# RMSNorm and matmul on one core: one token layout for loads and stores, a deeper prefetch, and one store cut at row 60

## The chip, the core and the metric

The kernel runs on one core of a Trainium2 chip. The metric is device time in microseconds (us), the median of several executions. "Span" is the length of one execution from its first to its last instruction; the timed figure of the same execution is about 1.8 us above it in every run here (the profiled one of the kernel before: span 210.9, time 212.7). An execution over 1.5% above the fastest of its kernel counts as slow. The engines: TensorE (PE) multiplies, VectorE (DVE) and ScalarE (ACT) do elementwise work, GpSimd (POOL) casts, SyncE (SP) issues transfers, and 16 DMA engines move the data.

## The reference, cut to what matters

```python
x: (16, 1024, 512) float32, gamma: 512 ones, weight: (512, 768) float32
rms = np.sqrt(np.mean(x ** 2, axis=-1, keepdims=True) + eps)
return np.matmul(x / rms * gamma, weight)          # (16, 1024, 768) float32
```

That is 16,384 tokens: 128 tiles of 128 tokens, in 16 groups of eight tiles. 33.6 MB are read and 50.3 MB written, and both TensorE and the DMA engines are nearly full.

## The kernel before

A tile's token sits in a partition, and a DMA of n tiles gives each of the 128 partitions n consecutive tokens. The same cutting of a group serves x and the output:

```python
AHEAD = 20
parts = {0: [1, 2, 1, 2, 2], 1: [4, 4], NG - 2: [4, 4], NG - 1: [2, 2, 2, 1, 1]}   # other groups: [8]
def rows(ap, i):
    return ap[first[i] * P:(first[i] + size[i]) * P, :].rearrange("(p t) d -> p t d", t=size[i])
xin  = ctx.enter_context(tc.tile_pool(name="xin", bufs=5))     # five groups of x
outp = ctx.enter_context(tc.tile_pool(name="out", bufs=3))     # three groups of output
def store(i):
    if i == first[i] + size[i] - 1:
        nc.sync.dma_start(out=rows(out, i), in_=held(o_tiles, first[i], size[i]))
# ... (casts, norms, transposes, matmuls left out)
warm_up(6); cast(0, nc.vector); square(0, ssq[:, 0:1]); transpose_tile(0); warm_up(3)   # start, on one line here
# ...
for j in range(2, NP):
    load_until(2 * j + AHEAD)
    # ... cast, norms, matmuls of tiles 2j and 2j+1, each followed by its store if the stretch is complete
```

All loads and stores are issued by SyncE in program order into one queue, which all 16 DMA engines work off. A store waits on SyncE for its last tile.

Of the kernel before, what the change touches and what calls it, by code (L numbers as in the profile page):

```python
# [18 lines left out]
def kernel(  # L19
# [8 lines left out]
    nc = tc.nc  # L28
    P = 128

    x = x.flatten_outer_dims()
    out = out.flatten_outer_dims()
# [3 lines left out]
    NT = N // P  # L36
    NP = NT // 2
    G = 8
    NG = NT // G
    AHEAD = 20  # L40
    WIDE = 512



    parts = {0: [1, 2, 1, 2, 2], 1: [4, 4], NG - 2: [4, 4], NG - 1: [2, 2, 2, 1, 1]}
    first, size = {}, {}
    for g in range(NG):
        i = g * G
        for n in parts.get(g, [G]):
            for t in range(n):  # L50
                first[i + t], size[i + t] = i, n
            i += n

    def rows(ap, i):
        return ap[first[i] * P:(first[i] + size[i]) * P, :].rearrange("(p t) d -> p t d", t=size[i])

    singles = ctx.enter_context(tc.tile_pool(name="singles", bufs=1))
    xin = ctx.enter_context(tc.tile_pool(name="xin", bufs=5))
# [8 lines left out]
    x_tiles, xb_tiles, tp_tiles, rstd_of, xT_tiles, o_tiles = {}, {}, {}, {}, {}, {}  # L67

    def held(tiles, i, n=1):
        return tiles[i // G][:, i % G:i % G + n, :]  # L70

    def load(i):
        if i // G not in x_tiles:
            x_tiles[i // G] = xin.tile([P, G, D], F32, name="xt")
        nc.sync.dma_start(out=held(x_tiles, i, size[i]), in_=rows(x, i))

    starts = [i for i in range(NT) if first[i] == i]

    def load_until(i):
        while starts and starts[0] < i:  # L80
            load(starts.pop(0))
# [52 lines left out]
    def accumulator():  # L134
        return opsum.tile([P, 2, WIDE], F32, name="ops").rearrange("p a b -> p (a b)")

    def out_tile(i):
        if i // G not in o_tiles:
            o_tiles[i // G] = outp.tile([P, G, O], F32, name="ot")
        return o_tiles[i // G][:, i % G, :]  # L140

    def store(i):
        if i == first[i] + size[i] - 1:
            nc.sync.dma_start(out=rows(out, i), in_=held(o_tiles, first[i], size[i]))

    def matmul(i, k, acc, lo, hi):
        nc.tensor.matmul(out=acc[:, lo:hi], lhsT=xT_tiles[i // 2][:, i % 2, k // 2, :, k % 2], rhs=w_bf[:, k, lo:hi],  # L147
                         start=(k == 0), stop=(k == K - 1))


    def matmuls(i, acc, ks, feed=None):
        for k in ks:
            matmul(i, k, acc, 0, WIDE)
            if feed:
                feed()
            matmul(i, k, acc, WIDE, O)

    def finish_tile(i, acc, engine):
        scale(engine, out_tile(i), acc[:, :O], rstd_of[i])
        store(i)  # L160
# [16 lines left out]
    with tc.manual_schedule():  # L177
# [9 lines left out]
        for h in range(2):  # L187
            nc.sync.dma_start(out=w_f32[:, 2 * h:2 * h + 2, :].rearrange("p c o -> p (c o)"), in_=wv[:, h, :])
        load_until(AHEAD)


        warm = singles.tile([P, WIDE], BF16)
        nc.vector.memset(warm, 0.0)  # L193
# [6 lines left out]
        def warm_up(n):  # L200
            for _ in range(n):
                nc.tensor.matmul(out=spare[:, :WIDE], lhsT=warm[:, :P], rhs=warm, start=True, stop=True)  # L202

        w_bf = singles.tile([P, K, O], BF16)

        def weights(k, engine, lo=0, hi=O):
            scale(engine, w_bf[:, k, lo:hi], w_f32[:, k, lo:hi], g_sb[:, k % 2, k // 2:k // 2 + 1])
# [21 lines left out]
        acc = [accumulator() for _ in range(4)]  # L229
        weights(0, nc.vector, 0, WIDE)  # L230
        weights(0, nc.vector, WIDE, O)
# [26 lines left out]
        for j in range(2, NP):  # L258
            load_until(2 * j + AHEAD)
            if j + 3 < NP:  # L260
# [19 lines left out]
        for i in (NT - 2, NT - 1):  # L280
            for lo, hi, engine in ((0, WIDE, nc.scalar), (WIDE, O, nc.vector)):
                a = accumulator()
                for k in range(K):
                    matmul(i, k, a, lo, hi)
                scale(engine, out_tile(i)[:, lo:hi], a[:, lo:hi], rstd_of[i])
            store(i)
# [35 lines left out]
```

## Time and profile before

| | before |
|---|---|
| median time | 211.38 us at first, 211.45 in the six runs beside the changed kernel |
| last matmul ends | 203.06 us |
| last store has landed, most engines / last engine | 206.7 / 210.0 us |
| end of the span | 210.9 us |

Read the table backwards, and note that the profiled execution was one of the slower ones (212.7 us). The span ends 0.9 us after the last engine, the last engine trails the others by 3.3 us, and the others are done 3.1 us after the last store was issued, at 203.6. The start and the end of TensorE's work, from the chain that ended last in order of time (start, duration, what):

```profile
0.74 2.87 DMA xt<-in_x_dram
...
7.45 1.40 PE ops L202 x6
8.85 2.61 PE ops L147 x16
...
197.41 5.65 PE ops L147 x35
```

The first tile of x lands at 3.61, six dummy matmuls that keep TensorE warm take 1.40 us, the real matmuls begin at 8.85 and the last piece ends at 203.06. The time from issue to landing (last column) of the large transfers:

```profile
out_dram<-ot SPq DMA_DIRECT2D x12, 3072.0 KB, 15.2
xt<-in_x_dram SPq DMA_DIRECT2D x12, 2048.0 KB, 19.6
```

### The profile page before, as it was taken

How to read it: one execution, taken by the hardware profiler on the slowest of the kernel's cores; microseconds unless marked ns; L12 is line 12 of the kernel's file. 1: busy time of each engine (PE TensorE's matmuls, PEld its weight loads, DVE VectorE, ACT ScalarE, POOL GpSimd, SP SyncE). 2: the span in 40 equal slices, each digit the busy share in tenths (PEclk: the TensorE clock that was granted, in tenths of full speed). 3: DMA queues.
4: the chain of work that ended last, by engine and by line, in shares of the span. 5: the costliest groups of instructions: out<-in, count | busy, mean ns of one | idle time of the engine just before them, and what ended most of it. 6: DMA issues, size and time to landing. Idle time of an engine off the chain costs nothing.

```text
span 210.9 us, 3573 instructions
## 1 busy us (share of the span) xinstructions
PE 199.8 (95%) x1272; PEld 138.0 (65%) x1297; DVE 111.6 (53%) x204; ACT 158.3 (75%) x388; POOL 66.2 (31%) x71
## 2 busy tenths in 40 slices
PE   7999999999999999999999999999999999999950
PEld 2466767766666777766667667766676777766620
DVE  2555654565456446645654565456546644654530
ACT  4589787778778877877787778777877887787720
POOL 1165512416233323332331333224143305050000
PEclk9999999999999999999999999999999999999996
DMA  6999999999999999999999999999999999999991
GB/s 228 408 428 423 398 398 420 418 419 431 441 407 427 437 437 412 438 435 406 447 418 441 416 432 438 364 435 429 432 418 437 418 451 383 422 440 378 392 376 78
DMA packets 8070, 85.69 MB, mean 406 GB/s; under 512 B 1138, under 2 KB 1140, under 8 KB 3956
## 3 DMA queue, kind: packets, MB, share of 16 engines
q1 hardware_dynamic: 7776, 85.46, 97.0%
q8 instruction: 10, 0.16, 0.3%
q10 hardware_dynamic: 276, 0.00, 0.1%
q14 instruction: 8, 0.07, 0.1%
HBM read 35.13 MB, written 50.33 MB: 405 GB/s over the span
## 4 chain that ended last, share of the span: by engine, by line
PE 92%; DMA 1%; DVE 1%; ACT 1%; issue 1%
PE ops L147 77%; PE tp L113 13%; DMA xt<-in_x_dram 1%; PE ops L202 1%; DVE ot L132 1%; ACT ot L130 0%; DVE xT L120 0%; ACT jk L90 0%; DVE xb L86 0%; PE tp L224 0%; ACT rms L94 0%; DVE rstd L96 0%
## 5 line engine op out<-in xcount | busy, mean ns | idle before, releaser
L147 PE MATMUL ops<-w_bf,xT 128*128 128x512 bf16 (+1 forms) x999 | 192.5, 324 | 1.4
L147 PEld LDWEIGHTS <-xT 128*128 128x128 bf16 x1024 | 100.2, 98 | 56.2 <-DVE xT L120 0.9
L86 POOL CAST xb<-xt 128x1024 bf16<-128x1024 f32 (+1 forms) x65 | 65.5, 1016 | 121.7 <-DMA xt<-in_x_dram 58.5
L120 DVE COPY xT<-tp 128x1024 bf16<-128x1024 bf16 (+1 forms) x67 | 44.5, 667 | 82.2 <-PE tp L113 82.2
L130 ACT ACTIVATE ot<-ops,rstd 128x768 f32<-128x768 f32 (+1 forms) x65 | 58.1, 894 | 38.6 <-PE ops L147 37.3
L90 ACT ACTIVATE jk<-xt 128x512 bf16<-128x512 f32 x128 | 78.8, 619 | 1.2 <-DMA xt<-in_x_dram 1.2
L113 PE MATMUL tp<-ident_f,xb 128*128 128x128 f32 x256 | 69.1, 275 | 0.4 <-DVE xb L86 0.3
L132 DVE TENSOR_SCALAR ot<-ops,rstd 128x768 f32<-128x768 f32 (+1 forms) x65 | 64.5, 992 | 2.9 <-PE ops L147 2.8
L113 PEld LDWEIGHTS tp<-ident_f,xb 128*128 128x128 f32 x256 | 36.0, 142 | 4.9 <-issue 1.1
L90 ACT ACTIVATION_READ_ACCUMULATOR jk<-xt 128x1 f32 x128 | 24.4, 190 | 0.0
L94 ACT ACTIVATE rms<-ssq,eps_sb 128x2 f32<-128x2 f32 (+1 forms) x64 | 18.9, 295 | 2.0
L96 DVE RECIPROCAL rstd<-rms 128x2 f32<-128x2 f32 (+1 forms) x64 | 9.9, 155 | 3.3 <-ACT rms L94 3.2
L202 PE MATMUL ops<-warm 128*128 128x512 bf16 x15 | 5.7, 531 | 1.2 <-DVE eps_sb L195 1.2
L202 PEld LDWEIGHTS <-warm 128*128 128x128 bf16 x15 | 1.7, 125 | 3.1 <-issue 1.4
L130 ACT ACTIVATE w_bf<-w_f,g_sb 128x768 bf16<-128x768 f32 x2 | 1.9, 936 | 1.4 <-DVE g_sb L226 1.4
L184 ACT ACT_TABLE_LOAD x1 | 1.3, 1283 | 1.8 <-issue 1.8
L86 DVE CAST xb<-xt 128x512 bf16<-128x512 f32 x2 | 1.1, 537 | 2.5 <-DMA xt<-in_x_dram 2.5
L132 DVE TENSOR_SCALAR w_bf<-w_f,g_sb 128x512 bf16<-128x512 f32 (+2 forms) x3 | 1.3, 475 | 0.0
L193 DVE MEMSET warm<- 128x256 uint32 x1 | 0.3, 272 | 0.9 <-PEq L303 0.9
L224 PE MATMUL tp<-ident_f,g_row 2*128 2x2 f32 x2 | 0.4, 265 | 0.3 <-DVE xT L120 0.3
L224 PEld LDWEIGHTS tp<-ident_f,g_row 2*128 2x128 f32 x2 | 0.3, 202 | 0.5 <-DVE xT L120 0.5
masks.py:199 POOL TENSOR_SCALAR_AFFINE_SELECT ident_f<-ident_f 128x128 f32<-128x128 f32 x1 | 0.3, 292 | 0.1
(7 smaller groups left out, 0.8 us busy)
## 6 DMA issues: line engine op xcount, KB each, us to landing
out_dram<-ot SPq DMA_DIRECT2D x12, 3072.0 KB, 15.2
xt<-in_x_dram SPq DMA_DIRECT2D x12, 2048.0 KB, 19.6
out_dram<-ot SPq DMA_DIRECT2D x4, 1536.0 KB, 11.8
out_dram<-ot SPq DMA_DIRECT2D x6, 768.0 KB, 9.4
xt<-in_x_dram SPq DMA_DIRECT2D x4, 1024.0 KB, 14.4
xt<-in_x_dram SPq DMA_DIRECT2D x6, 512.0 KB, 15.2
w_f<-in_weight_dram SPq DMA_DIRECT2D x2, 768.0 KB, 6.0
out_dram<-ot SPq DMA_DIRECT2D x4, 384.0 KB, 9.3
```

Of the source, the lines that this page charges most:

```text
L86: engine.tensor_copy(out=xb_tiles[i // 2][:, i % 2:i % 2 + n, :], in_=held(x_tiles, i, n))
L90: nc.scalar.activation(out=jk, in_=held(x_tiles, i)[:, 0, :], func=AF.Square, accum_out=ssq)
L94: nc.scalar.activation(out=rms[:, :n], in_=ssq[:, :n], func=AF.Sqrt, scale=1.0 / D, bias=eps_sb)
L96: nc.vector.reciprocal(out=rstd[:, :n], in_=rms[:, :n])
L113: nc.tensor.transpose(out=tp_tiles[j][:, t, h, :], in_=words[:, lo:lo + P], identity=ident_f)
L120: nc.vector.tensor_copy(out=dst[:, t:t + n, :], in_=src[:, t:t + n, :])
L130: nc.scalar.mul(out=dst, in_=src, mul=r)
L132: nc.vector.tensor_single_scalar(out=dst, in_=src, scalar=r, op=mybir.AluOpType.mult)
L147: nc.tensor.matmul(out=acc[:, lo:hi], lhsT=xT_tiles[i // 2][:, i % 2, k // 2, :, k % 2], rhs=w_bf[:, k, lo:hi], start=(k == 0), stop=(k == ...
L184: nc.scalar.preload_act_table(AF.Sqrt)
L202: nc.tensor.matmul(out=spare[:, :WIDE], lhsT=warm[:, :P], rhs=warm, start=True, stop=True)
L224: nc.tensor.transpose(out=gp[:, c, :], in_=g_row[:, :, c], identity=ident_f[:2, :2])
```

## The change

Its intent: every group has the same layout (partition p holds tokens 8p to 8p+7 of its group), so loads and stores may be cut differently; the last loads and first stores become larger; loads are issued a group earlier; and one store is divided unevenly over the DMA engines. The core of the diff:

```diff
-    AHEAD = 20
+    AHEAD = 28
+    MID = 5
-    parts = {0: [1, 2, 1, 2, 2], 1: [4, 4], NG - 2: [4, 4], NG - 1: [2, 2, 2, 1, 1]}
+    x_first, x_size = stretches({0: [1, 2, 1, 2, 2], 1: [4, 4]})
+    o_first, o_size = stretches({0: [4, 4], MID: [5, 3], NG - 2: [4, 4], NG - 1: [2, 2, 2, 1, 1]})
-        return ap[first[i] * P:(first[i] + size[i]) * P, :].rearrange("(p t) d -> p t d", t=size[i])
+        return ap.rearrange("(g p t) d -> g p t d", p=P, t=G)[i // G, :, i % G:i % G + n, :]
     def store(i):
-        if i == first[i] + size[i] - 1:
-            nc.sync.dma_start(out=rows(out, i), in_=held(o_tiles, first[i], size[i]))
+        first, n = o_first[i], o_size[i]
+        if i == first + n - 1:
+            uneven = first == MID * G + 5
+            for lo, hi in ((0, 60), (60, P)) if uneven else ((0, P),):
+                nc.sync.dma_start(out=rows(out, first, n)[lo:hi], in_=held(o_tiles, first, n)[lo:hi])
```

More of the change, by code (lines that the diff above doesn't have):

```diff
@@ L39, with stretches, rows @@
     NG = NT // G
-    AHEAD = 20
+    AHEAD = 28
     WIDE = 512
-    parts = {0: [1, 2, 1, 2, 2], 1: [4, 4], NG - 2: [4, 4], NG - 1: [2, 2, 2, 1, 1]}
-    first, size = {}, {}
-    for g in range(NG):
-        i = g * G
-        for n in parts.get(g, [G]):
-            for t in range(n):
-                first[i + t], size[i + t] = i, n
-            i += n
-    def rows(ap, i):
-        return ap[first[i] * P:(first[i] + size[i]) * P, :].rearrange("(p t) d -> p t d", t=size[i])
+    MID = 5
+    def stretches(parts):
+        first, size, i = {}, {}, 0
+        for g in range(NG):
+            for n in parts.get(g, [G]):
+                for t in range(i, i + n):
+                    first[t], size[t] = i, n
+                i += n
+        return first, size
+    x_first, x_size = stretches({0: [1, 2, 1, 2, 2], 1: [4, 4]})
+    o_first, o_size = stretches({0: [4, 4], MID: [5, 3], NG - 2: [4, 4], NG - 1: [2, 2, 2, 1, 1]})
+    def rows(ap, i, n):
+        return ap.rearrange("(g p t) d -> g p t d", p=P, t=G)[i // G, :, i % G:i % G + n, :]
     singles = ctx.enter_context(tc.tile_pool(name="singles", bufs=1))
@@ L74, in load @@
             x_tiles[i // G] = xin.tile([P, G, D], F32, name="xt")
-        nc.sync.dma_start(out=held(x_tiles, i, size[i]), in_=rows(x, i))
-    starts = [i for i in range(NT) if first[i] == i]
+        nc.sync.dma_start(out=held(x_tiles, i, x_size[i]), in_=rows(x, i, x_size[i]))
+    starts = [i for i in range(NT) if x_first[i] == i]
     def load_until(i):
```

## The prediction

> **What bounds the kernel now.** I read the page's busy table first, then its 40 slices, then the chain that ended last, then the stretch after the last matmul, then the DMA issues and who waits for DMA.
>
> ```profile
> PE 199.8 (95%) x1272; PEld 138.0 (65%) x1297; DVE 111.6 (53%) x204; ACT 158.3 (75%) x388; POOL 66.2 (31%) x71
> ...
> PE   7999999999999999999999999999999999999950
> ...
> DMA  6999999999999999999999999999999999999991
> ...
> q1 hardware_dynamic: 7776, 85.46, 97.0%
> ...
> PE 92%; DMA 1%; DVE 1%; ACT 1%; issue 1%
> ```
>
> Two resources are full at once: TensorE from slice 2 to slice 38, the DMA engines from slice 2 to slice 39. The chain names TensorE for 92% of the span, but the last two digits differ: TensorE is at 5 and 0 while DMA is at 9 and 1. The end is therefore a matter of stores.
>
> TensorE's pace is regular. In the chain in order of time four matmuls take 0.65 us and the transpose between fours 0.11, so a tile (eight matmuls, two transposes) takes 2 x (0.65 + 0.11) = 1.52 us and a group of eight 12.15; the stores of eight tiles are issued at 47.29, 59.43, 71.58, the same 12.15. The DMA records give the other pace: a packet is one partition's row of one DMA, 16,384 bytes of x take 611 ns at least (634.9 on average) and 24,576 bytes of output 912 (median). An engine has 8 of each per group: 4.89 + 7.30 = 12.19 us at best, 12.4 on average. So DMA is a little slower than TensorE and the queues carry a backlog.
>
> The cores' work after the last matmul (it ends at 203.06), in stretches; the columns after the engines' busy times are the granted clock, the DMA share of 16 engines, and GB/s:
>
> ```profile
> 199.00:204.00 5.00, 4.04 (x26) 2.21 (x23) 2.12 (x5) 2.27 (x3) 0.00 (x0) 1.00 0.88 361
> 204.00:206.00 2.00, 0.00 (x0) 0.00 (x0) 0.00 (x0) 0.00 (x0) 0.00 (x0) 1.00 0.99 399
> 206.00:207.00 1.00, 0.00 (x0) 0.00 (x0) 0.00 (x0) 0.00 (x0) 0.00 (x0) 1.00 0.39 151
> 207.00:208.00 1.00, 0.00 (x0) 0.00 (x0) 0.00 (x0) 0.00 (x0) 0.00 (x0) 0.85 0.14 55
> 208.00:209.00 1.00, 0.00 (x0) 0.00 (x0) 0.00 (x0) 0.00 (x0) 0.00 (x0) 0.50 0.09 37
> 209.00:210.00 1.00, 0.00 (x0) 0.00 (x0) 0.00 (x0) 0.00 (x0) 0.00 (x0) 0.50 0.04 15
> ```
>
> One sixteenth is 0.06. From 207 on only one to three of the 16 engines still move data; the rest are done. In the packet records the 16 completion marks of the last store are at 206.69 (first), 206.82 (ninth), 208.94, 209.07 and 210.02 (last); the span ends 0.9 us after that. The last engine can be followed back: its rows of the eight-tile stores take 931 to 1025 ns, mostly 954 to 964, where the others take 912 (about 90 of 1,536 packets, one engine's share being 96). It is about 5% slow on every store and carries its lag to the end.
>
> Who waits for DMA:
>
> ```profile
> POOL xb L86 <- DMA xt<-in_x_dram: 58.5, 20, 7.2
> ...
> PEld L147 <- DVE xT L120: 0.9, 2, 0.5
> ...
> ACT ot L130 <- DMA out_dram<-ot: 0.6, 1, 0.6
> ```
>
> GpSimd's casts wait for x 20 times, but nothing of it reaches TensorE: the weight loads waited 0.9 us in all. An output buffer was waited for once, 0.6 us.
>
> **What the Trainium skill says.** "DMA: Bandwidth & Descriptors", section "Why a DMA increments its semaphore by 16 and not by 1": a DMA issued from SyncE runs on the largest k up to 16 that divides the slowest dimension of both sides, on the lowest-numbered k engines. For 128 rows that is 16; for 60 it gives 15 engines with 4 rows; for 68 it gives 4 engines with 17 rows. The trace agrees for 128: 54 DMAs leave 54 x 16 = 864 completion marks and 8 packets per engine. Nothing in the trace tries 60 or 68. The same page, "Latency and other measured facts", says engines 7 and 15 are usually slower in traces, with an uncertain cause; this trace has one clearly slow engine but carries no engine numbers. That section also reports rates falling for row pitches of 512 KiB and more; the new loads have 16 KiB, which the page doesn't cover. "HBM Reference", section "Specifications (TRN2)", says that a core streaming alone measures about 425 GB/s; slices here show mostly 400 to 450.
>
> **The change part by part.**
>
> TensorE, VectorE, ScalarE and GpSimd keep the same instructions, in number and order. TensorE's 203.06 for the last matmul can move only by waits, and it has about 1.4 us of those outside the start.
>
> (1) Split loads. The last two groups of x come in one DMA each instead of 4+4 and 2+2+2+1+1 tiles, and group 0 is stored 4+4 instead of 1+2+1+2+2, group 1 in one. SyncE issues 21 loads for 26, and 25 stores for 26. Per engine, from mean packets: group 15's loads 3 x 8 x 0.164 + 2 x 8 x 0.09 = 5.4 us become 8 x 0.635 = 5.1; group 0's stores 2 x 8 x 0.122 + 3 x 8 x 0.237 = 7.6 become 2 x 8 x 0.466 = 7.5. With fewer marks, about 0.5 us less work per engine. It is worth something only on an engine still behind at the end.
>
> (2) The layout of eight consecutive tokens per partition everywhere. The first loads now read pieces of 2 to 8 KB at a pitch of 16 KB, where they read one whole block. Bytes and packet sizes are the same. If HBM likes it less, the first tile lands later than at 3.61 and TensorE's first matmul (8.85) slips. I take 0 to 0.3 us.
>
> (3) 28 tiles ahead. In SyncE's order each load already sits behind the store before it, so it is issued a whole group earlier, 12.15 us. GpSimd's waits for x should nearly vanish, and be worth nothing. Every store now queues behind one more load, 8 x 0.62 = 5 us: landing of eight-tile stores goes from 15.2 to about 20. An output buffer is needed again two groups and a tile later, about 25 us. That still fits, with 3 to 5 us left. Total bytes don't change, so the backlog at the end doesn't either.
>
> (4) The uneven store. Three tiles are 9,216 bytes per row; by the 24 KB packets that is 0.34 us. Normally each engine has 8 rows, 2.74 us. By the rule above the last engine gets none (-2.74, or -2.9 on the slow one), engines 4 to 14 get 4 rows (-1.37), and engines 0 to 3 get 21 rows, 13 more: +4.45 us. If the slow engine is the skipped one, it ends at 210.02 - 2.9 - 0.5 = 206.6, on the floor.
>
> The floor is set by TensorE: the last store is issued at 203.6 and the undisturbed engines finish it at about 206.7. With 0.9 us to close, that is a span of 207.6, 3.3 us below 210.9. The timed median lies 0.5 above the profiled span, so the floor in the metric is 208.1, -1.6%.
>
> Engines 0 to 3 eat into it. A fast engine's idle time between 193.3 and 206.7, between the last stores, is about 1 + 0.5 + 0.5 = 2 us. So 4.45 - 0.5 - 2.0 = 1.95 us stays beyond the floor for the fastest engine, plus its lag. At 193.3 the completion marks of a store show half the engines within 1 us of the first, four by 2 to 4.7 us behind. If 0 to 3 are fast ones: 208.1 + 1.95 + 0.2 = 210.3. If there is one of average lag among them: near 211.5. With fewer stalled reads (x packets average 24 ns over the best, 96 of them are 2.3 us per engine, most in the early stretch where reads and writes mix, and the deeper prefetch separates those) up to a microsecond comes back.
>
> **The rivals.** First: rows spread evenly. If 68 rows go over 14 engines with 5 each rather than over 4, nobody gets more than one extra row (0.34 us), the slow engine is relieved, and the time is on the floor, 208.1 to 208.4. Somebody chose 60 and 68 for a reason, which speaks for it; the skill's rule speaks against. Second: the overloaded engines become the bound. A laggard among engines 0 to 3, or the slow engine itself, ends 3 to 4 us later than now: 212 to 215. With 5 us from the load ahead and 4.45 more, stores would land after 25 us and output buffers would be waited for, so TensorE would show gaps. Third: strided small loads are slow, which would shift the start by one or several us; no row of this profile measures it. Fourth: the prefetch itself helps; TensorE's lack of waits speaks against it.
>
> **Range and chances.** I give the even spread 25% (208.2), overloaded engines that are otherwise fast 45% (209.3 to 210.5), overloaded engines with lag 25% (211 to 214), trouble at the start 5%. The middle is 209.8, the range 208.0 to 213.0. Faster by over 2% means below 207.15, under the floor that TensorE sets: 4%. Slower by over 2% means above 215.6: 8%.
>
> **What would show it right or wrong.** The matmul groups keep their means and TensorE its 12.15 us per group; the last matmul ends within 0.5 us of 203.06. The DMA share after 206 tells the rest: if it falls from 1 to 0 within a microsecond, the load is even; if 0.25 stays for some us, four engines are overloaded; if 0.06 stays, the slow engine was not the skipped one. The 60-row store should leave 15 completion marks, the 68-row one 4 or 14. Landing of eight-tile stores should be near 20 us, and GpSimd's waits for x fall from 58.5 to under 15. I am wrong if TensorE gains waits of over a microsecond, if the first matmul comes after 9.5, or if the last matmul comes earlier than 202.

## The result, and the profile after

The changed kernel took 214.36 us (212.49 to 214.91, six runs), the kernel before 211.45 beside it. The ratio is 1.0124, 95% interval 1.0084 to 1.0163. A ratio here is the mean time of one kernel's fast runs over that of the other's in the same rounds, so it is not quite the ratio of the medians. The change is slower by a little over 1%. The prediction held a change within 2% for the likeliest outcome, and that came, but the time lies outside its range of 208.0 to 213.0.

From the page of the changed kernel (span; busy times; slices of PE and DMA; the chain):

```profile
span 213.1 us, 3585 instructions
...
PE 202.7 (95%) x1297; PEld 138.5 (65%) x1297; DVE 111.6 (52%) x204; ACT 158.2 (74%) x388; POOL 66.6 (31%) x71
...
PE   6999999999999999999999999999999999999940
...
DMA  6999999999999999999999999999999998898991
...
PE 92%; DMA 2%; DVE 1%; ACT 1%; issue 0%
```

The averages look as before. (Busy PE is higher partly because the earlier trace lacked 25 matmul records.) The DMA row no longer holds 9 up to the end: in the last seven slices some engines run dry while others still work. The stretches after 204 show it (PE, weight load, DVE, ACT and POOL busy, granted clock, DMA share of 16 engines, GB/s):

```profile
204.00:206.00 2.00, 0.81 (x6) 0.39 (x4) 0.52 (x2) 0.69 (x1) 0.00 (x0) 1.00 0.97 393
206.00:207.00 1.00, 0.00 (x0) 0.00 (x0) 0.00 (x0) 0.00 (x0) 0.00 (x0) 1.00 0.95 383
207.00:208.00 1.00, 0.00 (x0) 0.00 (x0) 0.00 (x0) 0.00 (x0) 0.00 (x0) 1.00 0.98 393
208.00:209.00 1.00, 0.00 (x0) 0.00 (x0) 0.00 (x0) 0.00 (x0) 0.00 (x0) 0.74 0.36 141
209.00:210.00 1.00, 0.00 (x0) 0.00 (x0) 0.00 (x0) 0.00 (x0) 0.00 (x0) 0.50 0.23 92
210.00:211.00 1.00, 0.00 (x0) 0.00 (x0) 0.00 (x0) 0.00 (x0) 0.00 (x0) 0.50 0.11 46
211.00:212.00 1.00, 0.00 (x0) 0.00 (x0) 0.00 (x0) 0.00 (x0) 0.00 (x0) 0.50 0.05 22
```

A share of 0.23 is almost four engines of 16. Most engines are done at 208.5, four trail, the last until 212.2. The chain in order of time:

```profile
0.74 3.28 DMA xt<-in_x_dram
...
7.93 2.67 PE ops L211 x6
10.61 2.63 PE ops L156 x16
...
199.18 5.65 PE ops L156 x35
```

All of TensorE's work lies later than before. The first tile lands at 4.02, 0.41 later. The six dummy matmuls take 2.67 us for 1.40. The real matmuls begin at 10.61, 1.76 later, and end at 204.83, 1.77 later. Between those two points TensorE loses nothing. Landing times, and the waits that answer to those shown of before:

```profile
out_dram<-ot SPq DMA_DIRECT2D x12, 3072.0 KB, 23.6
xt<-in_x_dram SPq DMA_DIRECT2D x14, 2048.0 KB, 21.2
```

```profile
POOL xb L90 <- DMA xt<-in_x_dram: 13.2, 6, 4.1
...
PEld L156 <- DVE xT L124: 0.9, 2, 0.5
```

GpSimd's waits for x fell from 58.5 to 13.2 us, and it bought nothing. Eight-tile stores land 8.4 us later than before, where 5 had been reckoned.

Between the two profiles the end moved by 2.2 us (by the medians 2.9), and two things could account for it: TensorE's late start (1.8) or the four trailing engines. The experiments had to tell which.

In the DMA packet records 739 completion marks are counted: 45 transfers on 16 engines are 720, and 15 + 4 are the other 19. That fits a 60-row store on 15 engines and a 68-row one on 4, as the rule of the largest divisor says, and the share of 0.23 in the tail. The other cuts agree: rows 0 to 119 and 120 to 127 left 23 marks in experiment 3 (15 + 8), and the cuts at 64 and 113 left 38 in experiments 11 and 12 (16 + 7 + 15).

### The profile page after: what moved, and what is told of

The parts are those of the page before. It is cut to its first block, busy times and chain, and to the rows that moved or that the text cites. A ratio compares the mean times of both kernels' runs of the same rounds, so it can differ in the third digit from the quotient of the medians.

```text
span 213.1 us, 3585 instructions
## 1 busy us (share of the span) xinstructions
PE 202.7 (95%) x1297; PEld 138.5 (65%) x1297; DVE 111.6 (52%) x204; ACT 158.2 (74%) x388; POOL 66.6 (31%) x71
## 4 chain that ended last, share of the span: by engine, by line
PE 92%; DMA 2%; DVE 1%; ACT 1%; issue 0%
PE ops L156 77%; PE tp L117 13%; PE ops L211 2%; DMA xt<-in_x_dram 2%; DVE ot L136 1%; ACT ot L134 0%; DVE xT L124 0%; ACT jk L94 0%; DVE xb L90 0%; PE tp L233 0%; ACT rms L98 0%; DVE rstd L100 0%
## 5 line engine op out<-in xcount | busy, mean ns | idle before, releaser
L156 PE MATMUL ops<-w_bf,xT 128*128 128x256 bf16 (+1 forms) x1024 | 194.1, 326 | 0.1
L211 PE MATMUL ops<-warm 128*128 128x512 bf16 x15 | 7.0, 629 | 1.2 <-DVE eps_sb L204 1.2
```

What stands on the lines that cost most here:

```text
L156: nc.tensor.matmul(out=acc[:, lo:hi], lhsT=xT_tiles[i // 2][:, i % 2, k // 2, :, k % 2], rhs=w_bf[:, k, lo:hi], start=(k == 0), stop=(k == ...
L211: nc.tensor.matmul(out=spare[:, :WIDE], lhsT=warm[:, :P], rhs=warm, start=True, stop=True)
```

## The experiments

The kernel before took 211.57 us in experiments 1 to 4, 211.84 in 5 to 8 and 211.19 in 9 to 12, the three batches on three different chips, so compare ratios across them, not times. Medians and ranges count every execution. All results were correct.

**1. The three-tile store whole.**

```diff
-            uneven = first == MID * G + 5
+            uneven = False
```

> The changed kernel with the three-tile store whole. Theory (the loss is two things: a start later by 1.8 us, and four engines overloaded by the 68-row store): the real matmuls still begin near 10.6 and end near 204.8, but the tail has only the one slow engine, which lies 3.3 - (1.8 - 0.4) - 0.5 = 1.4 us past the floor, so the span falls from 213.1 to about 210.8 and the time from 214.4 to about 212.1. Rival 1 (all of the loss is the late start, the split costs nothing): stays at 214.4. Rival 2 (all of it is the split): 211.4 or less, and the start back at 8.85.

Measured: 212.04 us (211.45 to 212.91), ratio 1.0026 (0.9991 to 1.0061). The tail of its profile, in the columns of the stretches above:

```profile
206.00:207.00 1.00, 0.00 (x0) 0.00 (x0) 0.00 (x0) 0.00 (x0) 0.00 (x0) 0.50 0.14 55
207.00:208.00 1.00, 0.00 (x0) 0.00 (x0) 0.00 (x0) 0.00 (x0) 0.00 (x0) 0.50 0.07 28
208.00:209.00 1.00, 0.00 (x0) 0.00 (x0) 0.00 (x0) 0.00 (x0) 0.00 (x0) 0.50 0.02 9
```

From 207 on the share is one engine's, as before the change. The time is the expected one, but not all of its working is: in this profile the real matmuls began at 8.47, not 10.6, though the layout was the new one. The late start is therefore not a fixed property of the layout. Undoing the split alone takes the ratio from 1.0124 to 1.0026, most of the loss.

**2. Group 0 loaded and stored the old way, the split kept.** Group 0 uses contiguous blocks of 1, 2, 1, 2, 2 tiles for both x and output.

```diff
+        if i < G:
+            return ap[i * P:(i + n) * P, :].rearrange("(p t) d -> p t d", t=n)
-    o_first, o_size = stretches({0: [4, 4], MID: [5, 3], ...
+    o_first, o_size = stretches({0: [1, 2, 1, 2, 2], MID: [5, 3], ...
```

> The changed kernel with group 0 loaded and stored in the old way (contiguous blocks of 1, 2, 1, 2, 2 tiles); the 60/68 store stays. Theory: the first tile lands at 3.6 again, the real matmuls begin near 8.9 and end near 203.1, but the four overloaded engines don't care about TensorE's start, since their backlog sets their end: the time falls only by the 0.4 us that the loads start earlier, to 213.5 to 214.0, and four engines still end 3 to 5 us after the rest. Rival 1 (start is everything): 212.6 or less, the full 1.8 us. Rival 3 (the start differs from run to run, not by the layout): matmuls begin at 10.6 here too.

Measured: 217.89 us (216.21 to 220.01), ratio 1.0273 (1.021 to 1.0336). This missed in the wrong direction: the real matmuls began at 8.70 as expected, and the kernel became slower, not faster. The list of waits (total us, times, longest) shows what is new in it:

```profile
ACT ot L136 <- DMA out_dram<-ot: 15.6, 6, 3.3
```

ScalarE waited six times for an output buffer whose store had not landed (stores took up to 27.5 us), and the last matmul ended at 204.27 although it had started early. With the split a TensorE that starts early ran into the buffers here. That is not yet what made the kernel slower: most engines were done at 208.0, and a few trailed to 213.3 (DMA share 0.13 between 209 and 210, 0.12 between 211 and 212), so stores set the end again, not the matmuls. Why they trailed further than in the changed kernel is not shown. "Start is everything" is refuted.

**3. The cut at row 120.** By the divisor rule 15 engines take 8 rows each, then 8 engines one more, and only the last engine is left out.

```diff
-            for lo, hi in ((0, 60), (60, P)) if uneven else ((0, P),):
+            for lo, hi in ((0, 120), (120, P)) if uneven else ((0, P),):
```

> The changed kernel with the three-tile store cut at row 120 in place of 60: by the rule of the largest divisor 15 engines get 8 rows, then 8 engines one more, the last none. Theory: no engine has more than one row extra (0.34 us), the slow one is relieved of 2.9 us, the DMA share falls from 1 to 0 within a microsecond of the last store, and the span is start-bound: floor 208.5 + 0.3 + 0.9 = 209.7, time near 211.0. Rival (the slow engine isn't the last one): one engine still trails by 1.5 to 3 us, time 212 to 213.

Measured: 212.19 us (211.24 to 212.61), ratio 1.0015 (0.9978 to 1.0052). The overload is gone. One engine still trailed, landing at 209.9 where the rest were done at 208.4: the rival's sign. The slow engine is not the one that the cut leaves out. In this profile the matmuls began at 10.42 and ended at 204.63, so here the late start did set the floor. It is the converse of experiment 8 below: with TensorE as late as in the changed kernel, but even shares, the loss was gone.

**4. Both: old group 0 and the cut at 120.**

> Both repairs: group 0 in the old way and the cut at row 120. Theory: the floor that TensorE sets, 206.7 + 0.3 + 0.9 = 207.9 of span, time 208.4 to 208.9, ratio 0.986 to 0.988, matmuls from 8.9 to 203.1. Rival (start and tail overlap, one of the repairs is worthless): the same time as the better of the two single repairs.

Measured: 211.55 us (211.38 to 212.14), ratio 1.0005 (0.9977 to 1.0032). The matmuls ran from 8.89 to 203.10, most engines were done at 206.8, one only at 208.7. The expected 208.4 to 208.9 was missed for two reasons: that engine kept trailing, and the floor had been put 1.3 us too low (see below).

**5. The split alone, in the kernel before.**

```diff
-        if i == first[i] + size[i] - 1:
+        if i // G == MID:     # 5 tiles, then 3 tiles as rows 0 to 59 and 60 to 127
+            ...
+        elif i == first[i] + size[i] - 1:
```

> The kernel before with one thing of the change: the output of group 5 stored as five and three tiles, the three cut at row 60. Start, layout and prefetch are the old ones. Theory (the 68-row store loads four engines with 13 rows more, 4.45 us at 347 ns a row, and slow rows on top, of which they can absorb about 2 us before the end): four engines trail at the end, 213.0 to 215.0, with no wait for output buffers since stores land 5 us sooner than in the changed kernel. Rival (the split hurts only together with the deeper prefetch): 211.0 to 212.0, at most one engine trailing.

Measured: 217.43 us (216.2 to 221.37), ratio 1.0223 (1.0188 to 1.0259). The split alone costs about 2%, and the time lies over the expected range. With 20 tiles ahead it hits the loads. The waits, where "PEld tp" is TensorE loading tiles to be transposed:

```profile
POOL xb L87 <- DMA xt<-in_x_dram: 88.8, 19, 10.5
...
PEld tp L114 <- POOL xb L87: 5.4, 8, 1.8
```

The loads queued behind the overloaded engines arrive late, GpSimd casts late, and TensorE starves: its last matmul ended at 206.40 though it began at 8.20. At the end only one engine trailed, to 215.4, where four had been expected.

**6. 28 tiles ahead alone, in the kernel before.** (AHEAD = 20 becomes 28.)

> The kernel before with 28 tiles ahead instead of 20, nothing else. Theory: same time within 0.5 us (211.1 to 212.1); eight-tile stores land about 5 us later (near 20), GpSimd's waits for x fall from 58 to under 20 us, and TensorE doesn't notice. Rival (the prefetch itself costs, by output buffers that come free too late): over 213, with ScalarE or VectorE waiting for stores.

Measured: 211.81 us (211.36 to 214.49), ratio 1.0037 (0.9972 to 1.0103): no difference shown. Landing and waits moved as the theory said:

```profile
out_dram<-ot SPq DMA_DIRECT2D x12, 3072.0 KB, 19.9
```

GpSimd's waits for x fell to 11.8 us. The 4.7 us that stores land later is about the 5 us reckoned for one more load in the queue, and no engine waited for an output buffer.

**7. 20 tiles ahead, in the changed kernel.** (AHEAD = 28 becomes 20.)

> The changed kernel with 20 tiles ahead. Theory: the overloaded engines set the end whatever the order of loads and stores, so 213.5 to 214.9 as with 28. Rival (prefetch and split together are the cause): 212.2 or less.

Measured: 216.38 us (215.64 to 222.2), ratio 1.0215 (1.0179 to 1.0251). Without the deep prefetch the changed kernel is slower still, by about 2 us. GpSimd waited 85.0 us for x. The rival, that prefetch and split hurt together, is refuted; the prefetch softens what the split does to the loads.

**8. Eight dummy matmuls in the first batch instead of six, in the changed kernel.**

> The changed kernel with eight warm-up matmuls in the first batch instead of six, which fills TensorE's idle 0.69 us before the first transposes. If the late rise of TensorE's speed (six warm-up matmuls at 0.45 us each instead of 0.23) comes from that gap, the last warm-up batch takes 1.4 us again and the real matmuls begin at 9.4 or earlier instead of 10.6. The time falls little, 0 to 1 us, since the four engines set the end. Rival (the rise comes at a time of its own, whatever TensorE does): the last batch may again take 2.4 to 2.7 us.

Measured: 215.1 us (213.3 to 217.87), ratio 1.0138 (1.0087 to 1.0189). In its profile TensorE starts in time and the tail is as late as ever:

```profile
8.95 2.61 PE ops L156 x16
...
197.50 5.65 PE ops L156 x35
```

```profile
207.00:208.00 1.00, 0.00 (x0) 0.00 (x0) 0.00 (x0) 0.00 (x0) 0.00 (x0) 0.50 0.26 108
208.00:209.00 1.00, 0.00 (x0) 0.00 (x0) 0.00 (x0) 0.00 (x0) 0.00 (x0) 0.50 0.25 104
209.00:210.00 1.00, 0.00 (x0) 0.00 (x0) 0.00 (x0) 0.00 (x0) 0.00 (x0) 0.50 0.16 65
210.00:211.00 1.00, 0.00 (x0) 0.00 (x0) 0.00 (x0) 0.00 (x0) 0.00 (x0) 0.50 0.13 52
211.00:212.00 1.00, 0.00 (x0) 0.00 (x0) 0.00 (x0) 0.00 (x0) 0.00 (x0) 0.50 0.08 34
```

TensorE's last matmul ends at 203.15, as in the kernel before, but four of 16 engines (0.26, 0.25) work on, and the last store lands at 212.3 against 212.2. The 1.8 us of the late start were worth nothing in the changed kernel: the four engines set its end. This is the run that decides between the two candidates. It is one profile, but the timed runs agree that nothing was gained: 1.8 us less would have been a ratio near 1.004, and the interval begins at 1.0087.

**9. The cut at row 64, in the changed kernel.** A control: also two stores, but 16 divides both.

> The changed kernel with the three-tile store cut at row 64 in place of 60, so two stores as before, but each of 64 rows, which 16 divides: four rows and four rows for every engine. Theory (the uneven shares are the cause, not the cutting): as with the store whole, 211.5 to 212.5, and one engine trailing by about 2 us. Rival (a store of fewer than 128 rows is itself slow, whatever the shares): rows of this store take well over 347 ns on average and the time stays above 213.

Measured: 212.74 us (212.34 to 213.21), ratio 1.006 (1.0028 to 1.0092). Even shares take away about half of the loss (1.0124 to 1.006). Cutting itself costs up to 0.7 us against the whole store. Part of it may be the start, which was late in this profile (10.57), so this isn't settled.

**10. Old group 0 and the store whole.**

> The changed kernel with group 0 in the old way and the three-tile store whole: what is left of the change is 28 tiles ahead and the whole last loads. Theory: matmuls from about 8.9 to 203.1 in every run, one slow engine trailing by 2 to 3 us: 211.0 to 211.8, no different from the kernel before. Rival (the strided start costs its 1.8 us in most runs): 0.5 us or more below the run with the whole store and the new start (212.04).

Measured: 211.74 us (211.12 to 212.84), ratio 1.0025 (0.9986 to 1.0064). What remains of the change (deeper prefetch, whole last loads, the layout of the other groups) is worth nothing measurable.

**11 and 12. Cuts at rows 64 and 113**, tried in the kernel before and in the changed one with old group 0. The 49 rows in the middle go to seven engines.

```diff
+            for lo, hi in ((0, 64), (64, 113), (113, P)) ...
```

> The kernel before with the three-tile store of group 5 cut at rows 64 and 113: 16 engines with 4 rows, 7 engines with 7, 15 engines with 1. Engines 0 to 6 get 12 rows, 7 to 14 get 5, the last 4. It asks which of engines 4 to 7 is the slow one: five rows if it is number 7, twelve if it is 4, 5 or 6. Theory with number 7: it is relieved by three rows, 1.1 us, the others' four rows more (1.4 us, if they take 347 ns) fit into their slack of 2 us, time 210.3 to 211.0. Rival: narrow stores cost double rows as in the changed kernel, or the slow engine is below 7: 212.5 to 214.

> The same three cuts (64, 113) with 28 tiles ahead, whole last loads and the old start. If the relief works, this has the better prefetch on top and is the best version: 209.5 to 210.8. Rival: as for the cuts with 20 tiles ahead, 212 or more, or no different from the run without cuts (211.0 to 211.8).

Measured: 214.66 us (213.4 to 215.43), ratio 1.0152, and 213.82 us (212.35 to 214.56), ratio 1.0109. Both are slower, the trailing engine worse: in the second it landed at 211.2, the rest at 206.9. The rival held. No version that I tried beats the kernel before.

**Which engine is slow?** The packet records carry no engine number. A row of a store can be linked to the next where one starts as the other ends, and the slow engine's rows stand out, here at 354 to 371 ns for the 9,216 bytes that take others 347. In experiment 8 such a chain has exactly four rows and then a load, so the slow engine took part in the 60-row store and not in the 68-row one: 4 to 14. In experiment 3 it has eight rows and one more: 0 to 7. In experiment 12 slow rows run on into the 49-row store: 0 to 6. If engines are filled from the lowest number up, and if it is the same engine each time, that is 4, 5 or 6 together. But the three experiments ran on three different chips, and no run shows that the slow engine has the same number on each. This is reading, not a measurement by itself.

## Why the prediction was right or wrong

*What bounds the kernel.* Right. TensorE paced the middle in every run without the split, and the end was a matter of stores and of one slow engine.

*Part (1), fewer and larger transfers; part (3), the deeper prefetch.* Right in worth: nothing. Experiment 10 has both, experiment 6 has the prefetch alone. The 5 us of later landing were 4.7 alone. In the changed kernel they were 8.4, since the overload came on top (with the store whole, in experiment 1, stores land after 19.8 us, 4.6 later). (The stores are 24, not the 25 that the prediction counted.)

*Part (2), the layout.* The first tile landed 0.41 later in the changed kernel, against the 0 to 0.3 I took. A consequence was missed: TensorE idled longer before its first transposes, and its speed rose late. In the five profiles with the new layout and the original warm-up the real matmuls began at 8.47, 9.14, 10.42, 10.57 and 10.61; in the eight with the old group 0 between 8.20 and 9.07. The three late ones are those in which TensorE sat idle 0.69 to 0.80 us before its first transposes; the other two have 0.53 and 0.54. The prediction had named a first matmul after 9.5 as a sign of its being wrong. The Trainium skill, "TensorE: Matmul & The Clock Gate", section "Part 1: The HAM clock gate (the "warmup" mystery)", says that TensorE's rate doubles after a busy window of about 3.4 us which runs on its own, so that the moment varies from run to run. The traces agree with the doubling (0.45 us per dummy matmul, then 0.23) and with the variation. That filling the idle gap cures it rests on the one profile of experiment 8. In any case this was not the loss: there the start was early and the end as late.

*Part (4), the uneven store. This is the step that failed, in three terms; a fourth lies in the floor.*

The first is "If the slow engine is the skipped one". It was not. By its linked rows it kept four of its eight, and the engine left out was an ordinary one. Even so its last row of the eight-tile stores ended at 191.4, where it had been 194.4 before, so it is not what the tail waits for.

The second is the overload, "13 more: +4.45 us". The count of rows was right, 4 + 17 per engine on four engines, by marks and by the quarter of the engines in the tail. The time per row was too small. I took 347 ns throughout. In the changed kernel 22 of the 128 rows took 425 to 1,589 ns, all of them begun at 101.07 or later, when 83 rows had started, and the rows together took 9.38 us more than 347 ns each. If all of that fell on the four engines it is 2.3 us for each: by this estimate the term comes to about 4.45 + 2.3 = 6.8 us.

Why the rows were slow is not shown. Eight of the 22 lie between 671 and 734 ns, near two times 347, and others near three and more (1,118, 1,589), which looks like two or more engines taking turns. It would fit the page "SBUF — State Buffer", section "Door 1: The DMA port swizzle (why `[64,N]` ≈ `[32,N]`)": memory partitions are reached through 16 ports, and the 68-row store gives four engines partitions of many ports. Stores that were cut in other ways also had 10 to 17 rows over 400 ns (11 in experiment 9, with even shares, so slow rows don't need overloaded engines), the whole three-tile stores of experiments 1 and 10 one and none. No run tests the ports, and they leave open why the first rows of the changed kernel ran at the usual time.

The third is what it does to the rest. "That still fits, with 3 to 5 us left" was said of output buffers before the overload. With it the buffers were waited for, 15.6 us in experiment 2 and 4.9 in experiment 8. With 20 tiles ahead it was the loads that came late (experiments 5 and 7).

The fourth is a slip in the floor. The prediction put the timed figure 0.5 us above the span by comparing a median with the span of one slower execution; for the same execution it is about 1.8 in every run here (the profiled one of the kernel before: span 210.9, time 212.7). The floor "in the metric" was thus not 208.1 but 207.6 + 1.8 = 209.4, and the gain to be had about 2 us, not 3.3. With both terms put right the prediction's own sum, 209.4 + 6.8 - 0.5 - 2.0, gives 213.7 for engines without lag; the measured 214.36 leaves 0.7 for it. That is bookkeeping by estimates, not a separate measurement. One reading of the lags was off too: the last of the 16 marks of the store near 193.3 came 5.5 us after the first, not 4.7.

*The rivals.* The one that came true is the second, overloaded engines as the bound, to which I gave 25% with lag and 45% without. Its end came true, not the gaps in TensorE that it foresaw: in the changed kernel the matmuls lost nothing between the first and the last. The even spread, with 25%, is refuted by the marks. It had pulled the middle down to 209.8: an argument from "somebody chose 60 and 68 for a reason" against a stated rule.

What stays open: why experiment 2 is so much slower than experiment 8 when both start early (they ran on different chips); which of the overloaded engines trails; and whether the cut itself costs anything at even shares.

## What to carry to other kernels

When the DMA engines are full, rows per engine are a load like any other: work out what each engine gets, and give no engine more than it can absorb before the end. A cut that relieves one engine must first know which one is slow, and what it costs the others at the row time of the cut store, not of the whole one. A change that delays the compute engine may be hidden behind a later tail: before repairing a delay, ask in the tail which of the two ends last.

## What the Trainium skill lacked or had wrong

- "DMA: Bandwidth & Descriptors", section "Why a DMA increments its semaphore by 16 and not by 1": its divisor rule held for shapes that it doesn't list: 60 and 68 rows left 19 completion marks together (15 + 4), 120 and 8 rows 23 (15 + 8). It gives no cost of such a shape: here cutting one store into 60 and 68 rows cost 1% (the changed kernel against experiment 1) to 2.5% (experiment 2 against 10, on two chips) of the whole time.
- The same page, section "Latency and other measured facts", names engines 7 and 15 as usually slower, and gives as its best guess, called uncertain, a cause specific to descriptors that GpSimd writes. Here SyncE issued all the large transfers, and one engine was 5% slow in stores (954 to 964 ns for 24,576 bytes, the others 912). By its row counts, as read above, it was number 15 on none of the three chips (experiments 3, 8 and 12), and not number 7 on that of experiment 12, if engines are filled from the lowest number up.
- No page has row times of a store that is cut by partitions. Single rows took two to four times their usual time here (347 ns becoming about 700 and up to 1,589): 22 of 128 in the changed kernel, 11 of 128 with the cut at row 64.
- The row on large pitches in HBM, same page and section, starts at 512 KiB. At a pitch of 16 KiB with 2 KiB rows, ScalarE's first square, which waits for the first tile, began at 3.88 to 4.16 us in the six profiles of the new layout, against 3.29 to 3.67 in the eight with the contiguous block.
